# The last norm's residual added on GpSimd and VectorE, and the background work of a fused block re-laned

## The chip, the cores and the metric

The kernel runs on one core of a Trainium2 chip. The metric is the device time of one execution, in microseconds (us); the kernel before has a median of 2214.71 us over three runs (2211.72 to 2218.50). TensorE is called PE in the views of the profile, VectorE DVE, ScalarE ACT, GpSimd POOL, and SyncE, which issues most of the transfers, SP. An engine's name with a "q" behind it is its sequencer, and "L252" is line 252 of the kernel before.

## The reference

One layer over 2048 tokens of 1024 channels, in float32:

```
h = rmsnorm(x, norm_mix_pre)
u_pool, u_glu, g_a, g_b = split(h @ w_in)                 # 512, 2 x 512, 1024, 1024 columns
A = (pool_mixer(u_pool) * pool_scale) @ w_pool_out        # trailing means over 2/4/8/16 frames minus the frame,
                                                          # a 128x128 map per group
v = causal_depthwise_conv(a * sigmoid(gate), width 31) + conv_b
B = silu(layernorm(v, conv_ln_g, conv_ln_b)) @ w_conv_out
merged = sigmoid(g_a) * A + sigmoid(g_b) * B
x = x + rmsnorm(merged @ w_o, norm_mix_post)
h = rmsnorm(x, norm_mlp_pre)
f = square(relu(h @ w_up)) @ w_down                       # 4096 hidden channels
out = x + rmsnorm(f, norm_mlp_post)
```

## The kernel before

**Tiles.** Channels lie on the 128 partitions. The tokens are two halves (b = 0 and 1) of 1024, each of two blocks of 512 (t = 0 and 1). A *cell* is a tile of 128 partitions by 1024 columns: 512 tokens of two groups of 128 channels. A cell has 512 KB, and so has one operation's tile of weights.

**Matmuls.** Each float32 operand is split into a rounded part and a rest (`split`, `split_w`: a cast on ScalarE, a subtraction on VectorE), and three of the four products of parts are made. The large matrix products run as *octets*: eight block products are replaced by seven (forms i = 1 to 7), whose operands are sums and differences of weight tiles (`weight_parts`) and of cells (`token_parts`). One *product* is one form: 24 matmuls of 128 x 128 by 512, some 5.4 us of PE. Its `sink` takes the result out of one of three PSUM tiles, which `ps_mm` hands round.

**Order of the work.** The products are PE's main line. Everything else is background: generators (the convolution's 31 taps, LayerNorm, pooling, the norms' sums, the last weights) sit in `Lane`s. After each product `bg()` calls each lane once. A lane adds its rate to a credit and takes one generator step per unit; a bare `yield` ends a step, `yield n` ends the lane's turn and lets it pass over n - 1 further calls. So the rates and the numbers behind `yield` say how many products later a step is issued. The instructions' final order and the buffers are chosen by a scheduler of priorities: `tc.high_priority(offset)` lifts instructions ahead of others, and `behind()` ties a lane's instructions behind the main line. On each engine the instructions then run in that fixed order; SP's and POOL's transfers wait in it for what they depend on.

**Octets ahead.** `run_octets` goes through the jobs (octet, form), the first two octets interleaved as `START` says. Before each product it asks for the token parts of a later job with `parts.need`: the next one for the first four jobs, then two jobs ahead.

**Pools of tiles.** `big` has 28 tiles for cells, accumulators and token parts; `tr` has nine, which sinks, lanes and splits share; `fo` has five in the later stages; `wr` has four for raw weights, `wh` and `wl` three each for their parts. Where a weight's rest was kept from the first half (`kept`), or was made ahead for the last slab (`lows`), it is loaded into `wl` rather than computed.

**The stages, by the profile's clock:** inputs, the first octet and the projections of b = 0 (to about 306 us), branch A, the projections of b = 1 (350 to 632), the merge and output projection of b = 0, branch A of b = 1, `mlp_up` of b = 0 (814 to 1124), merge and output projection of b = 1, `mlp_up` of b = 1 (to 1577), and the down projection of both halves, with the last norm. Within them:

- `conv_steps` and `pool_steps` of b = 0 run in the lane `tail`, then in the second projections' first lane, followed by `norm_steps(0, 1)`. `conv_steps` of b = 1 waits until both are through.
- `norm_steps(b, lag)` is the LayerNorm. It loads the four cells `yd`, subtracts the mean, stores each cell again, and sums the squares; after the root it loads all four a second time, scales them, applies the sigmoid and stores `zd`.
- `pool_weights` multiplies the pooling's maps into `w_pool_out`; the maps' two parts are the constant tiles `pw`.
- `mlp_scale` makes the second norm's scale: it loads `x1d`, squares on ScalarE, adds on VectorE, and `root_acc` on PE sums over partitions (L458). Its lane runs beside `last_weights` in `mlp_up` of b = 1.
- The last norm has one `Finish` object per (b, t). `steps` squares the finished cells, `root_pe` and `root_dve` give the inverse root, `spread_pe` spreads it over partitions into `rb`; then each cell is multiplied by `rb` and x (`x1d`, in DRAM) is added. For b = 0 a POOL-issued transfer with `accum_op` adds `x1d` into the cell, and SP stores it. For (1, 1) two cells go that way and two have x loaded by `fetch` and added on VectorE. For (1, 0), in `at_end`, two outputs start as copies of `x1d` and get the cell added by a transfer into DRAM; the other two are added on VectorE, the last in halves.

The core of the way by transfer:

```
mul(two(y), two(y), per_token(self.rb))
...
nc.gpsimd.dma_start(y, x1d[self.b, c, self.t], accum_op=ALU.add)
load(out[self.b, c, self.t], y)
```

Of the kernel before, what the change touches and what calls it, by code (L numbers as in the profile page):

```python
# [15 lines left out]
P = 128  # L16
# [8 lines left out]
CW = 512  # L25
# [43 lines left out]
def block_kernel(  # L69
# [23 lines left out]
    p_wr = pool("pwr", 4)  # L93
# [838 lines left out]

    def norm_steps(b, lag):
# [21 lines left out]
        for c in range(CC):  # L955
# [3 lines left out]
            load(yd[b, c, 0], y[c])  # L959
# [14 lines left out]
        prefetch(0)  # L974
        yield 1
        sg = {}
        for c in range(CC + 1):
            if c < CC:
                if c + 1 < CC:
                    prefetch(c + 1)  # L980
# [8 lines left out]
            if c:  # L989
                mul(y[c - 1], y[c - 1], sg[c - 1])  # L990
                load(zd[b, c - 1, 0], y[c - 1])
            yield 1

    pw = [p_const.tile([P, CW], F32R, tag=f"pw{i}", name=f"pw{i}") for i in (0, 1)]
# [3 lines left out]
    def pool_weights():  # L998

        yield 2  # L1000
        raw = tr()
        load(raw[:, :CW], w_pool)
# [12 lines left out]
        for g, t in ahead_by_one(range(CC), get):  # L1015
            hi, lo = split(t, *TR)
            yield 3
# [354 lines left out]
    def mlp_scale(b, buf):  # L1372

        st = None
        for t in (0, 1):
# [10 lines left out]
            yield 1  # L1386
# [11 lines left out]
    def mlp_up(b, parts):  # L1398
        def one(u):
# [87 lines left out]
    def run(*octets):  # L1487
        run_octets([o for group in octets for o in group], bg)
# [5 lines left out]
    tail = Lane(1.3, conv_steps(0, (0,)))  # L1494
# [14 lines left out]

    def more():  # L1510
# [3 lines left out]
        tail.rate = 3  # L1514
# [3 lines left out]
    lanes.append(tail)  # L1518
    then(lambda: lanes.append(stats), o2, 5)
    run(  # L1520
        [o2],
        [then(more, pi, 3)],
        gate(0, parts, 3, sad, "ga", "lows"),
        gate(0, parts, 5, sbd, "gb", "sums"),
    )
# [21 lines left out]
    def pooling():  # L1547
        lanes[0].rate = 2.8
        lanes.append(Lane(1.4, marked(pool_steps(1, False), "pool")))
# [9 lines left out]
        gate(1, parts, 5, sbd, "gb", "sums"),  # L1559
    )  # L1560
# [33 lines left out]
    run(octs)  # L1594
# [191 lines left out]

    class Finish:
# [28 lines left out]
        def steps(self, lag):  # L1816
# [6 lines left out]
            if self.b and self.t:  # L1823
                self.fetch(self.order[2:])
# [12 lines left out]
            self.left = list(self.order)  # L1837
# [3 lines left out]
        def mul_left(self, n=4):  # L1841
            for c in self.muls[:n]:
                y = self.ready[c]
                mul(two(y), two(y), per_token(self.rb))
                if c not in self.x:
                    nc.gpsimd.dma_start(y, x1d[self.b, c, self.t], accum_op=ALU.add)
                    load(out[self.b, c, self.t], y)
                    self.left.remove(c)
            self.muls = self.muls[n:]
            self.add_left(0)  # L1850

        def add_left(self, n):
            for c in self.left[:n]:
                add(self.x[c], self.x[c], self.ready[c])
                load(out[self.b, c, self.t], self.x[c])
            self.left = self.left[n:]

        def first_squares(self):
# [207 lines left out]
```

## Time and profile before

| | |
|---|---|
| median of three runs | 2214.71 us (2211.72 to 2218.50) |
| the profiled execution | 2215.49 us |
| its span, first to last instruction | 2213.7 us |
| mean granted TensorE clock | 0.990 |
| PE busy | 2165.7 us, 9556 matmuls |
| VectorE, ScalarE, GpSimd busy | 1677.5, 1040.2, 20.6 us |
| transfers | 567.51 MB, mean 256 GB/s |

A row of the waits reads: engine, tile and line that waited, then what ended the wait, then total us, times and the longest. A row of the windows reads: stretch, its length, busy time and number of instructions of PE, weight load, VectorE, ScalarE and GpSimd, the mean granted clock, the transfers' busy share and GB/s. A row of the timeline reads: start, length, engine, line, operation, tiles out<-in, shape and how many were merged. Times are counted from the span's start.

### The profile page before, as it was taken

What the parts mean: (1) busy time and instruction counts of PE and PEld (TensorE: products, weight loads), DVE (VectorE), ACT (ScalarE), POOL (GpSimd) and SP (SyncE); (2) the same over time, 40 slices, a digit from 0 to 9 for tenths busy, and PEclk for the clock granted to TensorE, in tenths of its full rate; (3) what the DMA queues carried; (4) which work ended last, traced back from release to release, by engine and by line L of the source; (5) the groups of instructions that cost most, each with busy time, mean ns of one, the idle gap of its engine ahead of it and who ended that gap; (6) DMA issues with size and microseconds to landing.
All of it is one profiled execution on the core that took longest, in us unless ns stands there. A gap on an engine that the chain in (4) does not pass through costs nothing.

```text
span 2213.7 us, 25020 instructions
## 1 busy us (share of the span) xinstructions
PE 2165.7 (98%) x9556; PEld 1784.4 (81%) x9556; DVE 1677.5 (76%) x1633; ACT 1040.2 (47%) x1098; POOL 20.6 (1%) x39
## 2 busy tenths in 40 slices
PE   9999999999999999999999999999999999999996
PEld 7788787887888788888888877888888888888875
DVE  8998998987778888967657856876754656696667
ACT  5444353334533445456535766664554222223553
POOL 0000000000000000000000000000000000000001
PEclk9999999999999999999999999999999999999998
DMA  4779897678986688365686677985966545446798
GB/s 166 275 291 344 305 366 282 236 278 310 351 323 238 252 311 310 123 218 189 229 306 236 247 267 266 329 317 197 372 213 233 181 156 189 149 146 219 266 319 248
DMA packets 162791, 567.51 MB, mean 256 GB/s; under 512 B 18896, under 2 KB 23120, under 8 KB 162640
## 3 DMA queue, kind: packets, MB, share of 16 engines
q1 hardware_dynamic: 145968, 505.09, 64.1%
q10 hardware_dynamic: 12672, 46.14, 5.3%
q0 software_dynamic: 4032, 14.68, 2.5%
q8 instruction: 75, 1.23, 0.2%
q14 instruction: 44, 0.36, 0.0%
HBM read 376.49 MB, written 190.41 MB: 256 GB/s over the span
## 4 chain that ended last, share of the span: by engine, by line
PE 76%; DVE 9%; DMA 9%; issue 2%; ACT 2%; SPq 0%; DVEq 0%; ACTq 0%; POOL 0%; POOLq 0%
PE down L252 26%; PE up L252 22%; PE glu L252 6%; PE wo L252 6%; PE B L252 4%; PE A L252 4%; PE ga L252 3%; PE gb L252 3%; PE pool L252 2%; DVE y L918 2%; DVE wl L123 1%; DMA tr<-yd 1%; DVE tr L120 1%; DMA fo<-x1d 1%; DMA kept<-ws 1%
## 5 line engine op out<-in xcount | busy, mean ns | idle before, releaser
L252 PE MATMUL up<-big,wh 128*128 128x512 f32 x1792 | 482.4, 390 | 2.1 <-DVE big L123 1.8
L252 PEld LDWEIGHTS up<-big,wh 128*128 128x128 f32 x1792 | 337.0, 188 | 74.5 <-DVE big L123 3.9
L209 ACT CAST wh<-wr 128x1024 fp32r<-128x1024 f32 x169 | 177.5, 1051 | 324.1 <-PE up L252 77.8
L252 PE MATMUL down<-tr,wh 128*128 128x512 f32 x800 | 311.7, 390 | 0.0
L918 DVE SCALAR_TENSOR_TENSOR y<-v,cst,y 128x1024 f32<-128x1024 f32 x240 | 307.3, 1281 | 2.8
L252 PE MATMUL down<-fo,wh 128*128 128x512 f32 x784 | 301.8, 390 | 0.0
L252 PE MATMUL up<-big,wl 128*128 128x512 f32 x896 | 277.2, 390 | 0.0
L252 PE MATMUL down<-fo,wl 128*128 128x512 f32 x768 | 236.8, 390 | 2.9 <-DMA wl<-lows 2.9
L209 ACT CAST wh<-ws 128x1024 fp32r<-128x1024 f32 x118 | 124.2, 1052 | 221.8 <-PE up L252 84.1
L252 PEld LDWEIGHTS up<-big,wl 128*128 128x128 f32 x896 | 168.3, 188 | 34.7
L120 DVE TENSOR_TENSOR big<-big,down 128x1024 f32<-128x1024 f32 x88 | 106.8, 1218 | 111.9 <-PE down L252 104.0
L1727 ACT CAST fo<-tr 128x1024 fp32r<-128x1024 f32 x86 | 86.8, 1051 | 210.0 <-PE down L252 132.1
L252 PEld LDWEIGHTS down<-tr,wh 128*128 128x128 f32 x800 | 150.6, 188 | 31.2
L252 PEld LDWEIGHTS down<-fo,wh 128*128 128x128 f32 x784 | 147.5, 188 | 30.6
L252 PEld LDWEIGHTS down<-fo,wl 128*128 128x128 f32 x768 | 144.1, 188 | 33.2 <-DMA wl<-lows 3.3
L123 DVE TENSOR_TENSOR wl<-ws,wh 128x1024 fp32r<-128x1024 f32 x110 | 134.2, 1220 | 32.7 <-ACT wh L209 31.5
L123 DVE TENSOR_TENSOR wl<-wr,wh 128x1024 fp32r<-128x1024 f32 x99 | 120.5, 1218 | 27.9 <-ACT wh L209 26.8
L123 DVE TENSOR_TENSOR tr<-tr,fo 128x1024 fp32r<-128x1024 f32 x86 | 101.8, 1220 | 46.5 <-ACT fo L1727 46.5
L252 PE MATMUL wo<-big,wh 128*128 128x512 f32 x480 | 128.9, 390 | 0.0
L252 PE MATMUL gb<-big,wh 128*128 128x512 f32 x448 | 121.0, 392 | 3.0 <-DVE tr L120 2.4
L252 PE MATMUL glu<-big,wh 128*128 128x512 f32 x432 | 120.2, 400 | 3.5 <-DVE big L123 1.8
L252 PE MATMUL ga<-big,wh 128*128 128x512 f32 x448 | 120.9, 392 | 0.0
(197 smaller groups left out, 3349.1 us busy)
## 6 DMA issues: line engine op xcount, KB each, us to landing
tr<-fd SPq DMA_DIRECT2D x110, 512.0 KB, 4.6
wl<-kept SPq DMA_DIRECT2D x81, 512.0 KB, 4.8
kept<-wl SPq DMA_DIRECT2D x74, 512.0 KB, 5.7
wr<-w_down SPq DMA_DIRECT2D x68, 512.0 KB, 5.2
wr<-w_up SPq DMA_DIRECT2D x64, 512.0 KB, 4.6
wr<-w_in SPq DMA_DIRECT2D x56, 512.0 KB, 5.4
fd<-tr ACTq DMA_DIRECT2D x54, 512.0 KB, 3.6
fd<-tr SPq DMA_DIRECT2D x48, 512.0 KB, 3.5
```

What stands on the lines that cost most here:

```text
L120: return nc.vector.tensor_tensor(o, a, b, op=ALU.add)
L123: return nc.vector.tensor_tensor(o, a, b, op=ALU.subtract)
L209: nc.scalar.copy(hi[:, :n], src[:, :n])
L252: i = nc.tensor.matmul(ps, w[wp][:, (at + k) * P : (at + k + 1) * P], rhs[k][xp], start=start and n == 0, stop=stop and n == len(order) - ...
L918: nc.vector.scalar_tensor_tensor(acc, v[:, k : k + TB], wk, acc, op0=ALU.mult, op1=ALU.add)
L1727: nc.scalar.copy(hi, t)
```

## The change

1. *Last norm.* Every cell of the last norm now has x loaded by `fetch` on SP. Thirteen of the sixteen adds are `beside`, a GpSimd `tensor_tensor`; three are VectorE's (`order[1]`, `order[2]` and the halves of `order[3]` of (1, 0)). No transfer adds. For b = 0 the stores are issued by GpSimd, for b = 1 by SP.
2. *LayerNorm.* The last two cells, `HELD`, stay in their `tr` tiles between the two passes: they are neither stored nor loaded again, and the second pass begins with them. It asks for up to two cells ahead instead of one.
3. *Raw weights.* `wr` has five tiles. `pw` moves from the constants into a `tr` tile that `pool_weights` holds.
4. *Scale roots.* `mlp_scale` yields 2 instead of 1 between the sum and `root_acc`.
5. *Lanes.* `run_octets` asks three jobs ahead (from the fifth job, or from the fourth in the last `mlp_up`); the convolution's lane starts a product later at rate 1, `more` comes two forms later at rate 2.5; the second projections' lanes get rates 3.6 and 1.0; LayerNorm b = 1 has lag 3; `conv1` goes at 2.8; `pool_weights` waits 4; the last norm of b = 0 has rate and lag 3. The MLP sink's add is lifted by 60. `ahead[0]`, the lift of weight loads, is raised to 260 after `o2`'s first form.

```
-    p_wr = pool("pwr", 4)
+    p_wr = pool("pwr", 5)
...
-    def run_octets(octets, bg):
+    def run_octets(octets, bg, early):
...
-            o.run(i, jobs[min(n + (2 if n > 3 else 1), len(jobs) - 1)][1], bg)
+            o.run(i, jobs[min(n + (3 if n > early else 1), len(jobs) - 1)][1], bg)
...
+    HELD = (CC - 2, CC - 1)
     def norm_steps(b, lag):
...
-            load(yd[b, c, 0], y[c])
+            if c not in HELD:
+                load(yd[b, c, 0], y[c])
...
-        prefetch(0)
+        order = HELD + tuple(c for c in range(CC) if c not in HELD)
+        ready = list(HELD)
+
+        def ask(n):
+            if n < CC and order[n] not in ready:
+                prefetch(order[n])
+                ready.append(order[n])
+
+        ask(0)
         yield 1
         sg = {}
-        for c in range(CC + 1):
-            if c < CC:
-                if c + 1 < CC:
-                    prefetch(c + 1)
+        for n in range(CC + 1):
+            if n < CC:
+                c = order[n]
+                ask(n + 1)
+                ask(n + 2)
                 mul(y[c], y[c], r)
...
-    pw = [p_const.tile([P, CW], F32R, tag=f"pw{i}", name=f"pw{i}") for i in (0, 1)]
...
     def pool_weights():
...
         raw = tr()
+        both = mk(*TR, F32R)
+        pw = both[:, :CW], both[:, CW:]
...
             hi, lo = split(t, *TR)
-            yield 3
+            yield 4
...
     def mlp_scale(b, buf):
...
             ss = sq.total()
-            yield 1
+            yield 2
...
             def sink(m, t, ps, s):
...
-                    mark(add(o, ps, s))
+                    with tc.high_priority(offset=60):
+                        mark(add(o, ps, s))
...
-    tail = Lane(1.3, conv_steps(0, (0,)))
+    tail = Lane(1, conv_steps(0, (0,)))
...
+    def after_glu():
+        ahead[0] = AHEAD
+        lanes.append(tail)
...
     def more():
...
-        tail.rate = 3
+        tail.rate = 2.5
...
-    lanes.append(tail)
     then(lambda: lanes.append(stats), o2, 5)
     run(
-        [o2],
-        [then(more, pi, 3)],
+        [then(after_glu, o2, 1)],
+        [then(more, pi, 5)],
...
     def pooling():
...
-        lanes[0].rate = 2.8
-        lanes.append(Lane(1.4, marked(pool_steps(1, False), "pool")))
+        lanes[0].rate = 3.6
+        lanes.append(Lane(1.0, marked(pool_steps(1, False), "pool")))
...
-    conv1.gens.append(norm_steps(1, 2))
+    conv1.gens.append(norm_steps(1, 3))
...
     def faster():
...
-        conv1.rate = 3.4
+        conv1.rate = 2.8
...
+    def beside(o, a, b):
+        return nc.gpsimd.tensor_tensor(o, a, b, op=ALU.add)
...
-        def finish(self, c):
+        def finish(self, c, aside=False):
             y = self.ready[c]
             mul(two(y), two(y), per_token(self.rb))
-            if c in self.x:
-                x = self.x[c]
-                i = add(x, x, y)
-                load(out[self.b, c, self.t], x)
-                return i
-            else:
-                nc.gpsimd.dma_start(y, x1d[self.b, c, self.t], accum_op=ALU.add)
-                load(out[self.b, c, self.t], y)
+            x = self.x[c]
+            if aside:
+                beside(x, x, y)
+                (nc.gpsimd, nc.sync)[self.b].dma_start(out[self.b, c, self.t], x)
+                return
+            i = add(x, x, y)
+            load(out[self.b, c, self.t], x)
+            return i
...
         def steps(self, lag):
...
-            if self.b and self.t:
-                self.fetch(self.order[2:])
+            self.fetch(self.order[: 4 if self.b else 2])
...
-                for c in self.order:
-                    self.finish(c)
+                for n, c in enumerate(self.order):
+                    self.finish(c, True)
+                    self.fetch(self.order[n + 2 : n + 3])
                     yield
...
         def mul_left(self, n=4):
...
+                self.finish(c, True)
...
         def first_squares(self):
...
-            for c in self.order[:2]:
-                load(out[self.b, c, self.t], x1d[self.b, c, self.t])
-            for c in self.order[2:]:
-                self.x[c] = mk(*BIG)
-                load(self.x[c], x1d[self.b, c, self.t])
+            self.fetch(self.order)
...
         def at_end(self):
...
-                    fin[1, 1].add_left(1)
...
-                with behind():
-                    fin[1, 1].mul_left()
-                    fin[1, 1].add_left(4)
-                for c in self.order[:2]:
-                    y = self.ready[c]
-                    done = mul(two(y), two(y), per_token(self.rb)).ins
-                    nc.gpsimd.dma_start(out[self.b, c, self.t], y, accum_op=ALU.add)
+                self.finish(self.order[0], True)
+                self.finish(self.order[1])
                 done = self.finish(self.order[2]).ins
...
-    run(octs)
+    run(octs, early=2)
...
-                lanes += [Lane(2, fin[0, 1].steps(2), fin[0, 0].steps(2))]
+                lanes += [Lane(3, fin[0, 1].steps(3), fin[0, 0].steps(3))]
```

More of the change, by code (lines that the diff above doesn't have):

```diff
@@ L988, in norm_steps @@
                 )
-            if c:
-                mul(y[c - 1], y[c - 1], sg[c - 1])
-                load(zd[b, c - 1, 0], y[c - 1])
+            if n:
+                c = order[n - 1]
+                mul(y[c], y[c], sg[c])
+                load(zd[b, c, 0], y[c])
             yield 1
-    pw = [p_const.tile([P, CW], F32R, tag=f"pw{i}", name=f"pw{i}") for i in (0, 1)]
     w_pp = [dram("wpp", (P, D)) for _ in range(CPS)]
@@ L1485, in empty, with run @@
         lanes.clear()
-    def run(*octets):
-        run_octets([o for group in octets for o in group], bg)
+    def run(*octets, early=3):
+        run_octets([o for group in octets for o in group], bg, early)
     parts = Parts(first_parts)
@@ L1513, in more @@
         tail.gens.append(chain_of(pool_steps(0, True), conv_steps(0, (1, 2, 3), False)))
-        tail.rate = 3
+        tail.rate = 2.5
     pi = pool_in(0, parts, ahead_raw[1])[0]
     ahead[0] = 45
-    lanes.append(tail)
     then(lambda: lanes.append(stats), o2, 5)
     run(
-        [o2],
-        [then(more, pi, 3)],
+        [then(after_glu, o2, 1)],
+        [then(more, pi, 5)],
         gate(0, parts, 3, sad, "ga", "lows"),
         gate(0, parts, 5, sbd, "gb", "sums"),
+        early=3,
     )
@@ L1559, in block_kernel @@
         gate(1, parts, 5, sbd, "gb", "sums"),
+        early=3,
     )
@@ L1586, in block_kernel @@
     conv1.rate = 0.9
-    conv1.gens.append(norm_steps(1, 2))
+    conv1.gens.append(norm_steps(1, 3))
     lanes.append(conv1)
     def faster():
-        conv1.rate = 3.4
+        conv1.rate = 2.8
     octs = mlp_up(0, parts)
     then(faster, octs[1])
-    run(octs)
+    run(octs, early=3)
     empty()
@@ L1842, in mul_left @@
             for c in self.muls[:n]:
-                y = self.ready[c]
[L1844 to L1848, printed above, removed]
-            self.muls = self.muls[n:]
[L1850 to L1856, printed above, removed]
+                self.finish(c, True)
+            self.muls = self.muls[n:]
         def first_squares(self):
@@ L1933, in fill_cells, with filler @@
             fill[i] = token_cells(0, i, 0, (p_fo, "fo"))
-    def filler(part):
+    def filler(part, halves):
         for i in FIRST:
-            for o in (0, 1):
+            for o in halves:
                 w = part(i, o)
@@ L1958, in block_kernel @@
     lanes += [Lane(1, chain)]
-    filler(weights_down(0))
+    fw = weights_down(0)
+    filler(fw, (0, 1))
     octs = mlp_up(1, parts)
```

3 lines of the change are left out of this document (removed).

## The prediction

> **What bounds the kernel now.** I read the page first (busy shares and the chain that ended last), then what TensorE (PE) waited for, then the stretches around those waits, then the last 30 us.
>
> ```profile
> span 2213.7 us, 25020 instructions
> PE 2165.7 (98%) x9556; PEld 1784.4 (81%) x9556; DVE 1677.5 (76%) x1633; ACT 1040.2 (47%) x1098; POOL 20.6 (1%) x39
> PE 76%; DVE 9%; DMA 9%; issue 2%; ACT 2%; SPq 0%; DVEq 0%; ACTq 0%; POOL 0%; POOLq 0%
> ```
>
> PE is busy for 98% of the span, so 48 us are idle. The matmuls are not touched: the change can only move those 48 us, and what idle time does to the clock. The second view lists PE's waits, cause, total, times, longest:
>
> ```profile
> PE rb L458 <- DVE fo L120: 4.7, 3, 1.6
> PE glu L252 <- DMA wl<-kept: 4.0, 1, 4.0
> PE down L252 <- DMA wl<-lows: 2.9, 1, 2.9
> PE gb L252 <- DVE tr L120: 2.4, 2, 2.0
> PE up L252 <- DVE big L123: 1.8, 3, 0.8
> PE glu L252 <- DVE big L123: 1.8, 1, 1.8
> PE rb L458 <- DVE sm L120: 1.7, 1, 1.7
> PE glu L252 <- ACT big L202: 1.2, 1, 1.2
> ```
>
> They are a dozen separate causes; no engine but PE is a bound over the whole run. The third view gives stretches (us; PE busy; ... granted clock):
>
> ```profile
> 95.00:111.00 16.00, 12.75 (x42) 9.30 (x41) 14.66 (x14) 10.26 (x12) 0.00 (x0) 0.79 0.87 340
> 256.00:268.00 12.00, 9.97 (x37) 7.72 (x36) 11.96 (x11) 3.17 (x3) 0.00 (x0) 0.86 0.67 244
> 360.00:374.00 14.00, 9.98 (x37) 7.78 (x36) 8.96 (x8) 2.82 (x4) 0.00 (x0) 0.88 0.82 298
> ...
> 1365.00:1377.00 12.00, 10.39 (x43) 8.17 (x43) 8.81 (x8) 6.96 (x7) 0.00 (x0) 0.86 0.81 299
> ...
> 2126.00:2138.00 12.00, 9.08 (x34) 6.98 (x33) 2.33 (x3) 2.85 (x3) 0.00 (x0) 0.86 1.03 384
> ...
> 600.00:650.00 50.00, 50.00 (x222) 41.42 (x221) 35.94 (x31) 20.60 (x21) 0.00 (x0) 1.00 0.89 329
> ```
>
> The undisturbed row has 222 matmuls in 50 us, 4.44 per us. A stretch's loss is its idle time plus (1 - clock) times its length. 256 to 268: 2.0 idle + 0.14 x 12 = 1.7, so 3.7 us; by the count, 12 - 37/4.44 = 3.7 as well. In the same way 95 to 111 lost 3.25 + 3.4 = 6.6, 360 to 374 lost 4.0 + 1.7 = 5.7, 2126 to 2138 lost 2.9 + 1.7 = 4.6. So a wait of 2 us can cost 4: some waits take the clock down behind them.
>
> The Trainium skill's "TensorE: Matmul & The Clock Gate", in its table of why this matters, sets the limit at idle gaps of about 3 us; the trace disagrees, since the 2.0 us gap at 256 to 268 was followed by a clock of 0.86. By that rule only the 4.0 us wait would carry a clock term, and the sum below would come to some 2203 us.
>
> **The change part by part.**
>
> *Scale roots a call later* (`mlp_scale`, second `yield 2`). PE reaches `root_acc` before VectorE has finished the sum: 4.7 us in three waits, of at most 1.6 each; one took the clock down (1365 to 1377: 0.14 x 12 = 1.7). Together 6.4 us. One call is one product of 24 matmuls, 24/4.44 = 5.4 us, more than the longest wait. What is late next: the sum's `fo` buffer (one of five) comes free 5.4 us later, and the other lane's loads on SyncE (SP) queue behind that. Between 0 and -6.4 us; I take -5.5, near the full gain, because 5.4 covers 1.6 three times over.
>
> *Fifth raw weight buffer.* SP issues in order; its waits, and its issues ahead of the 4.0 us wait:
>
> ```profile
> SPq L129 <- ACT wh L209: 61.4, 56, 4.4
> SPq L129 <- DMA big<-x1d: 34.5, 8, 7.3
> ```
>
> ```profile
> 356.56 0.32 SPq L129 DMA_DIRECT2D wr<-kept  x1
> ...
> 359.40 0.32 SPq L129 DMA_DIRECT2D wr<-kept  x1
> 359.76 3.79 SPq L129 DMA_DIRECT2D wl<-kept  x3
> ```
>
> The `wl<-kept` that PE waits for stands on SP behind a `wr<-kept`, which waits until ScalarE's cast frees a raw buffer. With five buffers that load takes the one freed before 356.56, so the `wl` load goes out some 2.8 us earlier (359.40 - 356.56). That leaves about 1.2 of the 4.0 us, too little by the rows above to take the clock down. Gain 2.8 + 1.7 = 4.5; ends 0 (another wait on SP takes its place) and -5.7; I take -4. The buffer's memory is that of `pw`, which becomes a `tr` tile held during `pool_weights`; of that, the rivals.
>
> *Last norm of the first half* (`finish`, b = 0). The chain there:
>
> ```profile
> 2109.42 2.27 DVE big L126 x2
> ...
> 2112.43 10.64 DMA big<-x1d
> ...
> 2123.56 8.78 DMA wl<-lows
> ```
>
> An adding transfer takes 10.64 us, SP's store of its result waits for it, and `wl<-lows` behind that store comes 2.9 us late: 4.6 us lost. After the change the add is GpSimd's (POOL), and its store stands on POOL's queue, so SP is rid of the 34.5 us of waits above. What SP gets instead are the plain loads of x (`fetch`, two early, then one per step), which wait only for a `big` tile. Of 28, 16 are accumulators by then, 2 are `u`, 3 hold cells: free ones remain, so I cost these loads at nothing; if the cover goes, they block SP as the stores did. Ends 0 and -4.6; I take -4. `Lane(3)` and `steps(3)` move the same steps by a call or two, cost nothing while PE has products, and give the sums more time.
>
> POOL's price: no POOL arithmetic of this size is in the trace. Its nearest rows:
>
> ```profile
> L616 POOL CAST ident<-tr 128x128 fp32r<-128x128 f32 x1 | 0.3, 291 | 0.1
> ...
> L170 POOL MEMSET inv_d<- 128x1 f32 x1 | 0.1, 98 | 0.0
> ```
>
> (291 - 98)/128 = 1.5 ns a column; 1024 columns with one input 0.1 + 1.54 = 1.6 us, with two inputs up to twice that, 3.2. I estimate 2.4, the middle. There are 13 such adds (all four cells of three of the four `Finish`, one of the last), 31 us of an engine that is busy for 20.6 of 2213.7 us: hidden, except in the tail. The Trainium skill's "GPSIMD Engine Reference", section 3.1, has 4497 ns for twice the columns, so by estimate 2.3 us; the sum would be the same.
>
> *The tail.* After the last product VectorE works alone:
>
> ```profile
> 2188.46 2.35 DVE L126 TENSOR_TENSOR big<-big,rb 128x1024 f32<-128x1024 f32 x2
> 2190.72 1.22 DVE L120 TENSOR_TENSOR big<-big,big 128x1024 f32<-128x1024 f32 x1
> ...
> 2194.50 1.22 DVE L120 TENSOR_TENSOR big<-big,big 128x1024 f32<-128x1024 f32 x1
> 2195.67 3.48 DVE L126 TENSOR_TENSOR big<-big,rb 128x1024 f32<-128x1024 f32 x3
> 2199.19 1.22 DVE L120 TENSOR_TENSOR big<-big,big 128x1024 f32<-128x1024 f32 x1
> ...
> 2201.53 1.28 DVE L120 TENSOR_TENSOR big<-big,big 128x512 f32<-128x512 f32 x2
> ```
>
> ```profile
> 2189.26 1.95 PE L458 MATMUL rb<-inv_d,tr 128*128 128x1 f32 x16 [0.38 <-ACT tr L1889]
> ```
>
> ```profile
> 2208.00:2210.00 2.00, 0.00 (x0) 0.00 (x0) 0.00 (x0) 0.00 (x0) 0.00 (x0) 0.50 1.02 328
> 2210.00:2212.00 2.00, 0.00 (x0) 0.00 (x0) 0.00 (x0) 0.00 (x0) 0.00 (x0) 0.50 0.42 162
> ```
>
> ```profile
> DMA to landing us min/median/max: 4.0/9.2/11.6
> ```
>
> ```profile
> q1 hardware_dynamic: 1787, 6.65, 49.9%
> q0 software_dynamic: 818, 2.96, 43.9%
> ```
>
> The adds at 2190.72 and 2194.50 go to POOL; the first stood ahead of the root, which can begin when PE's sum is there (2189.26 + 1.95 = 2191.2) instead of at 2191.9: -0.7. The second ran while VectorE waited for PE's spread: nothing. Behind the root one add is new (order[1]): +1.1. VectorE ends some 0.4 us later, at 2203.2. The transfers, though, work at full share until about 2211, 8 us after VectorE's end at 2202.8: that backlog sets the end. From 2180 on the adding queue (q0) took 43.9% of 33.7 us for 2.96 MB, 5.0 us a MB, and the plain one (q1) 49.9% for 6.65 MB, 2.5 us a MB. Four adding transfers (0.52 MB each) and two copies of x1d leave; four plain loads and two plain stores come, and the other loads and stores stay. By these prices 10.5 + 2.6 us of transfer time go from the last 40 us and 7.9 come. So the last stores should land in 5 us (row: 4.0 at least, 9.2 at the median): at 2208.2 instead of 2202.8 + 9.3 = 2212.1. Ends +0.4 and -5; I take -4, near the fast end, as the backlog is what the change removes. POOL's five last adds fit: two by 2189, two by 2194.5, the last from 2196.8 to 2199.2; at 3.2 us each to 2200.3, still ahead of VectorE.
>
> *Parts and lanes in the first 300 us.* `run_octets` asks for token parts three jobs ahead from the fifth job on, not two: form 7, whose cells came late at 95 to 111, is asked for one job (5.4 us) earlier. By the lanes' rates, counted call by call, the convolution's first cell ends two calls later and its second not before the next input stage: some 17 taps fewer on a VectorE that is busy for 14.66 of 16 and 11.96 of 12 us there. They land where it is busy for some 36 of 50. At stake: 6.6 + 3.7, and the later `up<-big` waits of 1.8: 12. I take half, -6; ends 0 and -12.
>
> *LayerNorm keeps two cells.* Four 512 KB stores and four loads go away over both halves. PE waits for the LayerNorm only at its root (`sm`, 1.7 us), which follows the first pass, whose loads all stay: 0. `steps`, `in_stats` and the pool weights otherwise keep their instructions; `high_priority(60)` in the sink and the longer lags (LayerNorm 3, pool weights 4) order them differently: 0.
>
> *New waits.* The order from 55 to 1060 us is dealt out anew. I take +6, half of the largest of the groups above, with 0 and +13 as ends.
>
> Sum: -5.5 - 4 - 4 - 4 - 6 + 6 = -17.5 us. The profiled execution took 2215.5 us, its span and 1.8 around it, 0.8 above the median of 2214.7. 2215.5 - 17.5 = 2198.0, less 0.8: **2197 us**, 0.8% faster.
>
> **The rivals.** *The port.* VectorE's instructions with two inputs in SBUF might stand still while POOL adds. For it: in the tail two POOL adds fall on the root's small steps and one on the add of order[1]. The steps would wait from 2191.2 to 2192.0 and, where POOL's next add goes first, to 2194.4: 0.8 to 3.2 us, say 2. The add of order[1], due at 2198, would wait for POOL's to end at 2199.2: 1.2. The backlog's gain is then eaten: tail 0 instead of -4, elsewhere hidden under PE. 2201 us. No row of before shows POOL arithmetic beside VectorE. The Trainium skill's "SBUF — State Buffer", section "Who interferes with whom", states this rule (an exclusive lock against a GpSimd instruction that reads SBUF); no run here shows it yet.
>
> *A reshuffle.* The waits close where named, and as many open elsewhere: +18 instead of +6. For it: the waits of before have a dozen causes, none shared. Against: four are closed by construction. 2209 us, or no change.
>
> *Slower: `tr` runs out.* Nine `tr` tiles serve the sinks and the lanes. `pw` now holds one during `pool_weights` (about 20 calls), and the LayerNorm two over its lags (4 calls for b = 0, 10 for b = 1). If a sink finds none, its PSUM tile stays full, and PE stops: an idle time of 2 us costs 3.7 (256 to 268). From about seven such stops on (6.6 + 17.5 = 24 us) it decides; a stop in every third of those 34 calls, eleven, gives 2197 + 41 = 2238 us. Against it: the gap at 256, with `pool_weights` running, ended on VectorE's backlog rather than on a tile.
>
> **How the numbers follow.** About 0.3% (6.6 us) is what a measurement here tells from no change. Forecast 0.40, port 0.24, reshuffle 0.21, `tr` 0.15. Of the forecast and the port 0.63 is faster; the reshuffle splits toward no change: faster 0.65, same 0.20, slower 0.15. All gains at their ends with no new waits: 2214.7 - 6.4 - 5.7 - 4.6 - 5 - 12 = 2181. The range 2180 to 2217 leaves out most of the `tr` case and little below.
>
> **What would show it.** Right: no PE wait on `fo` at L458, none on `wl<-lows` in the first half's last norm, the `wl<-kept` wait under 1.5 us, fewer clock dips before 300 us; no adding transfer; last store landing within 6 us of VectorE's end. Wrong: PE waits on sinks' `tr` tiles around 150 to 250 or 900 to 1000 us; SP waiting for `big` tiles ahead of `wl`; VectorE's root chain, 2.6 us long before (2191.9 to 2194.5), stretched by POOL.

## The result, and the profile after

The changed kernel takes 2191.75 us in the median of four runs (2190.13 to 2191.93), the kernel before 2213.22 (four runs): a ratio of 0.9902, 95% interval 0.9884 to 0.9920, or 21.5 us less. Forecast were 2197 us, 17.5 less. A second measurement of the same kernel (`ctl_after`) gave 0.9914 (0.9897 to 0.9931), with six runs from 2189.4 to 2198.0. Below, 0.9908 stands for the change, the mean of the two.

The page of the profiled execution, which took 2191.9 us (span, busy shares, the chain that ended last):

```profile
span 2190.1 us, 25018 instructions
PE 2157.9 (99%) x9556; PEld 1782.2 (81%) x9556; DVE 1690.8 (77%) x1632; ACT 1039.3 (47%) x1098; POOL 46.0 (2%) x48
PE 87%; DVE 6%; DMA 4%; issue 2%; ACT 1%; SPq 1%; DVEq 0%; ACTq 0%
```

PE idles for 32 us instead of 48. Another 8 us are in its busy time, 2157.9 for 2165.7 with the same 9556 matmuls: the clock dips less. On the chain, transfers fall from 9% to 4%. PE's waits now (cause, total, times, longest):

```profile
PE rb L550 <- DVE sp L530: 5.1, 2, 3.3
PE rb L458 <- DVE tr L120: 3.6, 4, 1.2
PE glu L252 <- ACT tr L408: 2.9, 1, 2.9
...
PE down L252 <- ACT fo L1746: 1.1, 1, 1.1
...
PE down L252 <- DVE big L123: 0.8, 1, 0.8
PE rb L458 <- DVE sm L120: 0.7, 1, 0.7
```

The three largest that the prediction priced (`fo` at L458, `wl<-kept` and `wl<-lows`) are gone, but for 0.3 us of `wl<-kept` at another place. PE now waits longest for the spread of a root, for a sum of squares, and for ScalarE's copy of a PSUM tile (L408, in `held`). These are the rows of the same causes before; the first of them, 3.7 us on `tr`, is missing from the list in the prediction:

```profile
PE rb L458 <- DVE tr L120: 3.7, 3, 2.2
...
PE rb L550 <- DVE sp L530: 1.4, 2, 1.2
...
PE glu L252 <- ACT tr L408: 0.2, 1, 0.2
```

So the copy's wait is new, the spread's has grown, and the sum's is as long as it was. Next come the stretches that the prediction priced, a new one, and two where the sinks might have lacked `tr` tiles (columns as before; the eighth number, ahead of the two on transfers, is the clock). The changed kernel reaches the same matmuls earlier, by 2 us at 256 and by 20 at 2126, so the second to fifth stretches are moved by that much:

```profile
95.00:111.00 16.00, 15.20 (x59) 11.76 (x60) 15.07 (x15) 8.96 (x11) 0.00 (x0) 0.91 0.85 329
254.00:266.00 12.00, 12.00 (x54) 9.95 (x53) 11.82 (x11) 6.06 (x6) 0.00 (x0) 1.00 0.84 276
355.00:369.00 14.00, 14.00 (x63) 11.60 (x62) 7.38 (x6) 4.80 (x5) 0.00 (x0) 1.00 0.96 351
1350.00:1362.00 12.00, 12.00 (x59) 10.03 (x58) 10.58 (x10) 6.53 (x7) 0.00 (x0) 1.00 0.89 333
2105.00:2117.00 12.00, 12.00 (x58) 10.06 (x57) 11.86 (x10) 4.24 (x5) 4.00 (x4) 1.00 1.02 416
2156.00:2168.00 12.00, 9.60 (x42) 7.47 (x41) 8.31 (x16) 2.40 (x3) 5.29 (x3) 0.86 0.44 180
150.00:250.00 100.00, 100.00 (x443) 82.78 (x442) 84.39 (x88) 47.05 (x53) 0.00 (x0) 1.00 0.93 337
900.00:1000.00 100.00, 100.00 (x442) 82.80 (x441) 85.09 (x73) 55.10 (x56) 0.00 (x0) 1.00 0.43 160
```

Of the five that had lost time, four are undisturbed: full clock, and no idle time of PE. The first still loses 0.8 us of idle time and 0.09 x 16 = 1.4 of clock, and 2.9 us of idle time now lie just ahead of it. In the last two rows PE does not stop.

By the start of each stage's first matmul, the profiled time went thus. "Last matmul" is the last one of the last product of the down projection.

| from, to | before | after | difference |
|---|---|---|---|
| start, branch A of b = 0 | 306.7 | 300.6 | -6.1 |
| branch A, and two `pool` products of b = 1 | 54.4 | 55.7 | +1.3 |
| the other projections of b = 1 | 270.8 | 264.1 | -6.6 |
| B of b = 0 to the start of `mlp_up` of b = 1 | 624.3 | 622.1 | -2.1 |
| `mlp_up` of b = 1 | 320.4 | 312.0 | -8.4 |
| down projection, to the start of the last matmul | 610.3 | 612.3 | +2.0 |
| last matmul to the end | 26.8 | 23.3 | -3.6 |

The spans differ by 23.6 us: the profiled execution of before, 2215.5 us, stands 2.3 above the median of its four runs.

**The tail, and the port.** VectorE's instructions in the last 40 us (start, length, line, operation, tiles):

```profile
2152.64 2.99 DVE L502 TENSOR_SCALAR sy<-sa 128x4 int32<-128x4 int32 x1
...
2171.41 0.76 DVE L126 TENSOR_TENSOR s<-s,q 128x4 f32<-128x4 f32 x1
2172.20 2.29 DVE L500 TENSOR_SCALAR sa<-s 128x4 f32<-128x4 f32 x1
2174.53 0.17 DVE L502 TENSOR_SCALAR sy<-sa 128x4 int32<-128x4 int32 x1
...
2176.51 0.16 DVE L123 TENSOR_TENSOR sq<-sy,sp 128x4 fp32r<-128x4 f32 x1
2178.54 3.48 DVE L126 TENSOR_TENSOR big<-big,rb 128x1024 f32<-128x1024 f32 x3 [1.88 <-PE rb L550]
...
2185.59 1.28 DVE L120 TENSOR_TENSOR big<-big,big 128x512 f32<-128x512 f32 x2
```

and POOL's adds in the same time, then all of them in one group (total, mean ns):

```profile
2153.18 2.42 POOL L1807 TENSOR_TENSOR big<-big,big 128x1024 f32<-128x1024 f32 x1
...
2169.77 4.69 POOL L1807 TENSOR_TENSOR big<-big,big 128x1024 f32<-128x1024 f32 x2 [2.15 <-ACT tr L1894]
2179.90 2.36 POOL L1807 TENSOR_TENSOR big<-big,big 128x1024 f32<-128x1024 f32 x1 [5.43 <-issue]
```

```profile
L1807 POOL TENSOR_TENSOR big<-big,big 128x1024 f32<-128x1024 f32 x13 | 31.4, 2430 | 1337.2 <-DVE big L126 1323.2 <-issue 11.8 <-ACT tr L1894 2.1
```

In the kernel before, the first of the long steps was as short as its neighbours:

```profile
2192.24 0.17 DVE L500 TENSOR_SCALAR sa<-s 128x4 f32<-128x4 f32 x1
```

Lay the two timelines side by side. A step on four columns, 0.17 us before, took 2.29 us at 2172.20 and ended at 2174.49, when POOL's pair of adds ended (2169.77 + 4.69 = 2174.46). The one at 2152.64 ended at 2155.63, POOL's add there at 2155.60. So the root's chain in the tail lasts 5.5 us (2171.2 to 2176.7) where it took 2.7 before (2191.9 to 2194.6). The multiplications by `rb`, which have one input in PSUM, run at 3.48/3 = 1.2 us throughout. This is the rule of the Trainium skill's "SBUF — State Buffer", section "Who interferes with whom", and the trace agrees, for the one-input TENSOR_SCALAR as well as for the TENSOR_TENSOR of two SBUF inputs.

PE pays once more. It waits 3.3 us for the root, and the eight matmuls that spread it then take 1.9 us (2176.62 to 2178.5) where they took 1.1 before, and take 1.1 in `x_four` (below), where the wait is 0.6. The first of the eight in the changed kernel, then in `x_four`:

```profile
2176.62 0.39 PE L550 MATMUL rb<-ident,sp 128*128 128x128 f32 x1 [3.27 <-DVE sp L530]
```

```profile
2178.72 0.30 PE L550 MATMUL rb<-ident,sp 128*128 128x128 f32 x1 [0.56 <-DVE sp L530]
```

The stores make up for it. Transfers issued after 2182 (count, size, median us to landing):

```profile
out<-big SPq DMA_DIRECT2D x3, 512.0 KB, 2.8
out<-big SPq DMA_DIRECT2D x2, 256.0 KB, 2.1
```

VectorE ends 20.0 us after the start of the last matmul (2186.87 - 2166.86) instead of 15.9, which is +4.1: the root starts 0.6 earlier, its chain takes 2.7 more, the spread 0.8, and the one add more 1.2. From there to the end of the span it is 3.25 us (2190.12 - 2186.87) instead of 10.9, which is -7.6. Together -3.5.

### The profile page after: what moved, and what is told of

Read it like the earlier page. It is cut to its first block, busy times and chain, and to the rows that moved or that the text cites. A ratio compares the mean times of both kernels' runs of the same rounds, so it can differ in the third digit from the quotient of the medians.

```text
span 2190.1 us, 25018 instructions
## 1 busy us (share of the span) xinstructions
PE 2157.9 (99%) x9556; PEld 1782.2 (81%) x9556; DVE 1690.8 (77%) x1632; ACT 1039.3 (47%) x1098; POOL 46.0 (2%) x48
## 4 chain that ended last, share of the span: by engine, by line
PE 87%; DVE 6%; DMA 4%; issue 2%; ACT 1%; SPq 1%; DVEq 0%; ACTq 0%
PE up L252 27%; PE down L252 26%; PE wo L252 7%; PE ga L252 6%; PE glu L252 5%; PE B L252 4%; PE A L252 4%; PE gb L252 3%; PE pool L252 3%; DMA kept<-ws 1%; DVE tr L120 1%; DVE y L918 1%; DMA tr<-yd 1%; PE rb L458 1%; DVE wl L123 1%
## 5 line engine op out<-in xcount | busy, mean ns | idle before, releaser
L209 ACT CAST wh<-wr 128x1024 fp32r<-128x1024 f32 x169 | 177.7, 1052 | 324.9 <-PE up L252 85.2
L209 ACT CAST wh<-ws 128x1024 fp32r<-128x1024 f32 x118 | 124.2, 1053 | 216.2 <-PE up L252 92.0
L123 DVE TENSOR_TENSOR wl<-ws,wh 128x1024 fp32r<-128x1024 f32 x110 | 134.1, 1219 | 52.0 <-ACT wh L209 50.8
L123 DVE TENSOR_TENSOR tr<-tr,fo 128x1024 fp32r<-128x1024 f32 x86 | 101.8, 1219 | 42.4 <-ACT fo L1746 42.4
L123 DVE TENSOR_TENSOR wl<-wr,wh 128x1024 fp32r<-128x1024 f32 x99 | 120.4, 1217 | 10.9 <-ACT wh L209 8.8
```

The lines of the kernel that those rows point to most:

```text
L123: return nc.vector.tensor_tensor(o, a, b, op=ALU.subtract)
L209: nc.scalar.copy(hi[:, :n], src[:, :n])
```

## The experiments

Each ratio is against the kernel before on the same chip, so the changed kernel is the base at 0.9908 in all but `b_wr5`. An interval is some ±0.002, 4 us. The changed kernel itself ran on the same chip only with `x_copy`, `x_lag` and `x_all` (as `ctl_after`); for the other runs the ratio carries the base over from chip to chip.

| run | edit | median us | ratio (95%) | ratio less 0.9908, in us |
|---|---|---|---|---|
| `u_roots` | scale roots as before | 2198.64 | 0.9949 (0.9929 to 0.9969) | +9 |
| `u_wr4` | four raw buffers | 2213.26 | 1.0012 (1.0002 to 1.0022) | +23 |
| `u_norm` | last norm as before | 2196.31 | 0.9942 (0.9921 to 0.9962) | +8 |
| `u_lanes` | first lanes as before | 2206.28 | 0.9981 (0.9968 to 0.9994) | +16 |
| `u_ahead2` | parts two jobs ahead | 2193.34 | 0.9929 (0.9910 to 0.9948) | +5 |
| `u_held` | LayerNorm keeps none | 2198.69 | 0.9956 (0.9943 to 0.9969) | +11 |
| `x_four` | POOL's adds before the root | 2192.16 | 0.9918 (0.9898 to 0.9938) | +2 |
| `x_lag` | and b = 0's last norm earlier | 2199.56 | 0.9937 (0.9922 to 0.9952) | +6 |
| `x_copy` | `x_four`, copies lifted | 2186.34 | 0.9882 (0.9866 to 0.9898) | -6 |
| `x_all` | all three | 2196.79 | 0.9928 (0.9914 to 0.9943) | +4 |
| `b_wr5` | before, with five raw buffers | 2204.85 | 0.9981 (0.9969 to 0.9994) | (4 us faster than before) |

Taken out singly, six parts lose 72 us between them, of a gain of 20. They are not terms of a sum: what a part is worth depends on which others are there.

**Five raw buffers.** In the changed kernel:

```
-    p_wr = pool("pwr", 5)
+    p_wr = pool("pwr", 4)
```

> The changed kernel with four raw weight buffers instead of five. If the fifth buffer is what lets SP issue the kept weights' loads in time, the wait of PE on wl<-kept comes back in the second input projections (near 350 to 370 us), 4 us with a dip of the clock: 2191.8 + 5 = 2197 us. Rival: the new lanes alone took that wait away; then 2192 us, no wait on wl<-kept over 1 us, while SP's waits for ScalarE's casts grow by several us that nobody feels.

The whole gain is gone, but not where I had put it: from the pooling to the second `ga` this kernel takes 114.2 us, as the changed kernel does, and PE has no wait on `wl<-kept` over 0.3 us: the other edits close that wait without the buffer. It loses in the first run (+6), in `mlp_up` of b = 0 (+7) and of b = 1 (+7). Its waits on the copies of L408 are 16.9 us in all, 3.3 in the changed kernel; the largest row:

```profile
PE up L252 <- ACT tr L408: 7.7, 3, 3.9
```

and the chain that ended last around one of them (start, length, what):

```profile
862.37 10.88 DMA kept<-ws
...
873.26 1.24 DVE ws L123
...
875.48 1.04 ACT wh L209
876.52 0.92 ACT tr L408
...
877.48 4.60 PE up L252 x19
```

A store to DRAM (`kept<-ws`) takes 10.9 us. A sum on VectorE waits for it, a weight's cast on ScalarE for that sum, and behind the cast, in ScalarE's fixed order, stands the copy of a PSUM tile (L408) that PE needs back. No compute engine waits for a raw buffer at that moment; SP does, 9.5 us for the same sum, which reads one. The fifth buffer changes the order of the issues; that the casts' inputs thereby come earlier was not shown, and `ctl_after`, which has five buffers, has the same chain once (below). In the kernel before, the same edit alone:

```
-    p_wr = pool("pwr", 4)
+    p_wr = pool("pwr", 5)
...
-    pw = [p_const.tile([P, CW], F32R, tag=f"pw{i}", name=f"pw{i}") for i in (0, 1)]
...
+        both = mk(*TR, F32R)
+        pw = both[:, :CW], both[:, CW:]
```

> The kernel before with the fifth raw weight buffer alone (and the pooling maps in a tr tile, which pays for it). In the changed kernel, going back to four buffers cost some 20 us rather than the 4 predicted, and not at the wait that was named. If the buffer is worth that by itself, because ScalarE's PSUM copies stand behind casts whose raw weights come late, this run gains much of it: about 2197 us. Rival: the other edits ask for weights earlier and need the fifth buffer, which by itself is worth the 4 us of the prediction or nothing: 2207 to 2212 us.

Two of the stretches in this kernel:

```profile
1365.00:1377.00 12.00, 12.00 (x55) 9.94 (x53) 10.79 (x10) 8.74 (x10) 0.00 (x0) 1.00 0.58 206
360.00:374.00 14.00, 14.00 (x63) 11.43 (x62) 10.96 (x9) 4.06 (x5) 0.00 (x0) 1.00 0.99 385
```

The wait at 360 to 374 is gone, as forecast, and so are the waits on `fo` at 1365, which I had put down to the scale roots: `mlp_up` of b = 1 takes 313.9 us here instead of 320.4. So each of the two, the buffer alone and the other edits without it, closes the wait at 360. A new wait of 3.4 us on L408, at 167, gives part of it back.

**Scale roots as before.**

```
-            yield 2
+            yield 1
```

> The changed kernel with one edit undone: the scale roots are issued at once again (second yield of mlp_scale back to 1). If the later call is what hides the sums, PE waits on fo at L458 come back, some 4.7 us of idle time and one dip of the clock: 2191.8 + 6 = 2198 us, and the stretch from the first up product of b = 1 to the first down product is 6 us longer than with the change. Rival: the new order of the lanes hides the sums by itself; then 2192 us and no such waits.

`mlp_up` of b = 1 takes 312.8 us in its profile, 0.8 more than in the changed kernel, with a single wait on `fo` of 0.4 us: the waits did not come back. The time came out as expected all the same, but not by the path expected: the medians are 6 us above `x_four` on the same chip. The stages of the profiled execution, 4.8 us longer in all, differ both ways: 4.0 more in `mlp_up` of b = 0, where PE, VectorE and ScalarE have the order of the changed kernel, 1.8 more in the down projection, 4.6 less in the projections of b = 1. What the edit is worth, and by what path, stays open.

**Last norm as before.** `Finish`, its lane's rate and its lag are those of the kernel before:

```
-                lanes += [Lane(3, fin[0, 1].steps(3), fin[0, 0].steps(3))]
+                lanes += [Lane(2, fin[0, 1].steps(2), fin[0, 0].steps(2))]
```

> The changed kernel with the last norm as before (adding transfers, SP stores, rate and lag 2), all other edits kept. If the adds on GpSimd and the plain loads are worth what the tail and the wl<-lows wait cost, this run is 4 us longer between the last product and the end and waits again for wl<-lows: 2199 us. Rival, the port: VectorE lost about as much to GpSimd's adds (some 12 us of VectorE time, of which some 6 stood on the path) as the transfers cost; then 2192 to 2195 us, a shorter root chain (2.7 us instead of 5.5 us), and no wait of PE on that root's spread beyond 1.2 us.

The wait that the change removes is back:

```profile
PE down L252 <- DMA wl<-lows: 2.9, 1, 2.9
```

The tail takes 27.6 us instead of 23.3, the down projection 613.9 instead of 612.3. So this part is worth 4.3 + 1.6, some 6 us by the profile. With the adding transfers back, the last stores land late again (issued after 2180; median us to landing):

```profile
out<-big SPq DMA_DIRECT2D x5, 512.0 KB, 10.5
...
out<-big SPq DMA_DIRECT2D x2, 256.0 KB, 10.2
```

And without POOL's adds PE does not wait for the spread of (1, 1).

**POOL's adds before the root.** All four adds of (1, 1) go to POOL ahead of the root's steps:

```
             self.muls = list(self.order)
-            self.mul_left(2)
+            self.mul_left(4)
```

> The changed kernel, with all four products with the inverse root of (1, 1) made at once when the root is there, in the 3.4 us in which VectorE sits idle before the last product ends, instead of two then and two after it. GpSimd's third and fourth adds thereby end some 2 us earlier. If GpSimd's adds hold up VectorE's small root steps through a shared port, the last root takes some 3.3 us instead of 5.5, and the kernel ends 2 us earlier: 2190 us. Rival: the long TENSOR_SCALAR of 2.3 us there is a wait for something else (a semaphore, its first use); then it stays, and the time is 2192 us.

VectorE's steps at the root, and POOL's adds:

```profile
2176.42 0.17 DVE L500 TENSOR_SCALAR sa<-s 128x4 f32<-128x4 f32 x1
...
2178.61 0.16 DVE L123 TENSOR_TENSOR sq<-sy,sp 128x4 fp32r<-128x4 f32 x1
```

```profile
2166.88 9.38 POOL L1807 TENSOR_TENSOR big<-big,big 128x1024 f32<-128x1024 f32 x4 [6.34 <-issue]
```

POOL is through at 2176.26, the chain takes 2.7 us again, and from the last matmul to the end it is 19.8 us instead of 23.3. The root starts 4.35 us after the last matmul in both kernels, so the two multiplications that the edit moves as well were off the path. That isolates the port's price in the tail: 3.5 us, 2.7 of the chain and 0.8 of the spread. The time does not show it, as the profiled execution lost 3.4 us in the down projection: about 2.2 at its start (642 matmuls from 1550 to 1700 instead of 652; the same two waits of 1.2 and 0.8 us are followed by a clock of 0.88 over 14 us here, of 1.00 in the changed kernel), and 1.2 in a deeper dip of the clock (0.71 instead of 0.83 from 2160 to 2170) behind the wait of 1.8 us on the spread of (1, 1) that both kernels have.

**The last norm of b = 0 earlier**, to take POOL's adds away from that of (1, 1) as well (on top of `x_four`):

```
-                lanes += [Lane(3, fin[0, 1].steps(3), fin[0, 0].steps(3))]
+                lanes += [Lane(3, fin[0, 1].steps(2), fin[0, 0].steps(2))]
```

> The changed kernel with the four products of (1, 1) at once, and the last norm's steps of the first half issued with a lag of 2 products, not 3, so that GpSimd's adds of the first half should be over before the root of (1, 1) near 2152 us. If the port holds up that root (its TENSOR_SCALAR of 3.0 us) and PE waits 3 us for its spread, the wait goes and the root of the end is short too: 4 to 5 us less than the control. Rival: the adds fall on other VectorE work that PE waits for; then no better than 2 us less than the control, from the last root alone.

The rival was right. PE's largest row of waits, then VectorE and POOL around the longest one:

```profile
PE rb L458 <- DVE tr L120: 8.7, 5, 5.8
```

```profile
2140.84 2.50 DVE L123 TENSOR_TENSOR tr<-tr,fo 128x1024 fp32r<-128x1024 f32 x1 [0.88 <-ACT fo L1746]
2143.27 3.49 DVE L123 TENSOR_TENSOR tr<-tr,big 128x1024 fp32r<-128x1024 f32 x1
...
2153.48 4.54 DVE L120 TENSOR_TENSOR big<-big,big 128x1024 f32<-128x1024 f32 x2
```

```profile
2152.57 3.24 POOL L1807 TENSOR_TENSOR big<-big,big 128x1024 f32<-128x1024 f32 x1 [5.92 <-issue]
```

Two adds that take 1.2 us each take 4.54 together, and POOL's 3.24 instead of 2.4. Two subtractions, 1.2 us each otherwise, took 2.50 and 3.49 beside POOL's adds at 2139.84 and 2143.26. Together VectorE, which does not stop from there on, loses 5.7 us; PE waits 5.8 us for the sum of squares behind. Moved off one chain, the adds fell on another.

**The first lanes as before** (the rates, `tail`, `more`, the LayerNorm's lag, and weight loads lifted by 45 only until `more`):

```
-    tail = Lane(1, conv_steps(0, (0,)))
+    tail = Lane(1.3, conv_steps(0, (0,)))
...
-        lanes[0].rate = 3.6
-        lanes.append(Lane(1.0, marked(pool_steps(1, False), "pool")))
+        lanes[0].rate = 2.8
+        lanes.append(Lane(1.4, marked(pool_steps(1, False), "pool")))
```

> The changed kernel with the lanes' rates, starts and LayerNorm's lag of before, and with weight loads lifted by 45 only until the pooling octet's third form, all else kept (five raw buffers, three jobs ahead, the last norm, two cells held). If the thinner lanes are what relieves VectorE in the first projections, the matmuls up to branch A start 5 to 6 us later than with the change, and the wait on wl<-kept near 360 us may come back, since four raw buffers instead of five did not bring it back: 2191.8 + 6 to 10 = 2198 to 2202 us. Rival: asking three jobs ahead did it; then 2192 us and a first run as with the change.

The first run takes 315.7 us to branch A instead of 300.6, more than before the change (306.7). Two of its stretches, 165 to 177 and 296 to 308, each hold a wait for ScalarE, 3.4 us (L408) and 3.6 (L209), and have a mean clock of 0.72. `b_wr5`, with the old rates and five raw buffers, has the first of these waits but not the second, and reaches branch A at 308.7; so it is the old rates together with other parts of the change that cost 15 us. Which part was not tried.

**Parts two jobs ahead.**

```
-            o.run(i, jobs[min(n + (3 if n > early else 1), len(jobs) - 1)][1], bg)
+            o.run(i, jobs[min(n + (2 if n > 3 else 1), len(jobs) - 1)][1], bg)
```

> The changed kernel, asking for token parts two jobs ahead as before, all else kept. If the earlier request is what shortened the wait for form 7 near 95 to 111 us and the up waits near 1265 to 1290 us, these come back: 3 us in the first run, 2 us in mlp_up of b = 1, so 2197 us. Rival: the lanes did it; then 2192 us.

PE's order is unchanged. At 102.9 a wait of 2.2 us for `big` (L123) is back, the late cells that the prediction named, and two of 0.8 in `mlp_up` of b = 1; the first run is 1.8 us longer, that `mlp_up` 3.4. The intervals overlap, so the size, some 2 to 5 us, is not settled.

**LayerNorm keeps no cells.**

```
-    HELD = (CC - 2, CC - 1)
+    HELD = ()
```

> The changed kernel with no cell held in LayerNorm: all four are stored and loaded again, 4 MB more of transfers, and asking two cells ahead stays. Predicted worth of the held cells: 0, as PE waits only for the root that comes before: 2192 us. Rival one: the 4 MB delay what stands behind them on the full queues near 500 to 580 and 950 to 1050 us, by way of casts and copies behind late loads: 2195 us or more. Rival two: holding two of nine tr tiles costs; then it is faster, below 2189 us.

```profile
PE rb L458 <- DVE sm L120: 5.3, 1, 5.3
```

In the changed kernel this wait is 0.7. The load of the third cell is issued at 527.4, behind the first cell's store on SP, instead of 522.4. So the stores stand between the first pass's loads, and taking two away moves the root. That stretch, the projections of b = 1, is 5.2 us longer; the rest of the 11 us lies in later stages and was not traced.

**The copies lifted** (with `x_four`), after `u_wr4` had shown them waiting behind casts:

```
-            mark(nc.scalar.copy(s, ps))
+            with tc.high_priority(offset=300):
+                mark(nc.scalar.copy(s, ps))
```

> The changed kernel with the four products of (1, 1) at once, and ScalarE's PSUM copies (L408) lifted by 300 ahead of casts. If PE's waits on these copies come from casts that stand ahead of them on ScalarE and wait for late weights, the waits on L408 go (2.9 us near 95 us, and those near 290, 511 and 868 us): 3 to 6 us less than the control, 2187 us. Rival: the casts that fall behind are then late for PE in their turn; the time is that of the control or 2 to 5 us more, with new waits on wh or wl.

**The changed kernel again**, beside it: no edit.

> The changed kernel as it is, on the same chip as the next three, to see how far chip and execution move it: 2190 to 2195 us, with a profile whose waits agree with the first one to within 3 us at each place, apart from waits that end on ScalarE's PSUM copies (L408), which came and went near 868 us between runs of the same order of instructions.

Waits of the control, then of the kernel with both edits:

```profile
PE up L252 <- ACT tr L408: 3.2, 2, 3.0
...
PE glu L252 <- ACT tr L408: 2.5, 1, 2.5
```

```profile
PE pool L252 <- DVE wl L123: 1.8, 1, 1.8
...
PE ga L252 <- ACT tr L409: 1.1, 1, 1.1
```

It takes 2186.3 us (2184.3 to 2188.7), 6.6 less than the control and faster than either kernel. PE waits for its copies 1.1 us at most. At 95 us the waits that take their place, for the weights of `pool`, eat the gain; what stays is the tail of `x_four` and `mlp_up` of b = 0 (308.5 us, 313.4 in the control). The control's wait of 3.0 us there has the chain of `u_wr4`: a store of 10.1 us from 849.85 on, then a sum, a cast, and the copy at 863.23. It is not there in every execution: with the same order of instructions the changed kernel's first profile has 0.2 us in its place, and takes 308.3 us. So the order decides that PE can wait for a store's landing, and the landing decides whether it does. What the lift is worth alone is not shown: of the 5.3 us between the two profiles 3.5 are the tail's, which `x_four` has too, and the rest is this wait that comes and goes.

**All three:**

```
+            with tc.high_priority(offset=300):
+                mark(nc.scalar.copy(s, ps))
...
+            self.mul_left(4)
...
+                lanes += [Lane(3, fin[0, 1].steps(2), fin[0, 0].steps(2))]
```

> All three together (four products at once, copies lifted by 300, lag 2 for the first half's last norm). If both theories hold, 7 to 10 us less than the control, 2183 us. Rival: the copies' lift costs what it gives; then as the kernel with the lag alone.

Up to the down projection it is 2.7 us ahead of the changed kernel; its down projection then takes 621 us instead of 612, with the waits of `x_lag`. The time is the rival's; what brings it is the lag, not the lift.

## Why the prediction was right, and where its terms were not

The direction and, to 4 us, the size were right; several terms were not. That their sum came so near is partly luck: what was missed in one place (the down projection, 2.0 us longer instead of 4 shorter) was made up in others (8.4 instead of 5.5 in `mlp_up` of b = 1, 6.6 instead of 4 in the projections of b = 1).

- *Parts and lanes, -6 to 300 us.* Measured -6.1, and 256 to 268 is clear. But undoing the lanes costs 16 us: with the old rates, other parts of the change bring new waits.
- *Scale roots, -5.5.* The waits are gone, and `mlp_up` of b = 1 gained 8.4 us. The cause was wrong: `b_wr5`, which has the old roots, lost the same waits and gained 6.5 of it; `u_roots` did not get them back. Failed is the step that let one call's delay alone remove them.
- *Fifth raw buffer, -4 at 360 to 374.* The wait went, all 4.0 us and its dip, and alone the buffer is worth 4 us; but `u_wr4`, without the buffer, does not have the wait either. And the buffer counts for the whole gain when it is taken out. The step treated a buffer as one wait on SP; taking it out moves some 90 of SP's 997 issues and 46 of ScalarE's 1098 instructions to other places in their order.
- *Last norm of the first half, -4.* The wait on `wl<-lows` went (-4.6), but the down projection is 2.0 us longer. New there: 1.9 us at its start (`down<-fo` and `down<-big`, of which `b_wr5` has both too), 3.6 in three waits around the root of (1, 1), and 1.7 of clock at 2156 to 2168. The middle one, 1.8 us for the spread, is the port's: the stretched step at 2152.64, 2.8 us too long, stands in that chain, and `u_norm`, without POOL's adds, has no such wait. "Hidden, except in the tail" was the failing step.
- *The tail, -4.* Measured -3.6 as a sum of two sizes that I had otherwise: VectorE +4.1 for +0.4, the landings -7.6 for -4.4. The port rival's mechanism was real; its price for the chain, 2 us of 0.8 to 3.2, was 2.7, and the slower spread, which it did not name, cost 0.8. Its second charge, 1.2 us for the add of `order[1]`, did not come: POOL's add was over at 2182.26, and the two adds at 2181.94 took 2.52. The rival did not decide, because the last stores land in 2.1 to 2.8 us, faster than the 4.0 that I took as the least.
- *POOL's price, 2.4 us of 1.6 to 3.2.* Measured 2.43, 31.4 us in all as forecast.
- *LayerNorm's cells, 0.* `u_held` lost 11 us. I had counted the loads of the first pass and overlooked the stores between them on SP; that accounts for 5.2 us of it.
- *New waits, +6.* In the place of the waits named came 2.9 us ahead of 95, 1.3 in branch A and the 7.2 of the down projection above: 11.4, for a term of +6.
- *The clock.* Shallow waits carried dips and went with them: a third of the 23.6 us is PE's busy time (-7.8), that is clock, and not idle time.
- *`tr` runs out.* PE is busy for all of 150 to 250 and 900 to 1000, so this rival was empty.

## What to carry to other kernels

Where a fixed order on each engine couples everything, price an edit by what its engine's queue does in it, and do not add single undo runs up: the buffer, the lanes and the kept cells each cost more to remove than their share. Before adds are moved to GpSimd, list VectorE's serial chains of small steps; put the adds before or after them, and check what they fall on next. Where PE waits for a PSUM copy, look at what stands ahead of the copy on its engine: the run with the copies lifted and the adds before the root was the fastest here, 6.6 us under the control.

## What was not expected of the hardware

- A step on 128 x 4 elements took 2.3 or 3.0 us instead of 0.17, until POOL's add ended; adds and subtractions of 128 x 1024 lost 1.3 to 2.3 us in the same way.
- At the end, stores of 512 KB landed in 2.8 us and of 256 KB in 2.1 where no adding transfer ran beside them; with the adding transfers back (`u_norm`) it was 10.5 and 10.2.
- The same order of instructions gave 0.2 or 3.0 us of wait at one place in two executions, and stages 5 us apart.
- The clock did not follow the wait's length alone: waits of 1.2 and 0.8 us were followed by a clock of 0.88 over 14 us in one kernel and by no dip in another with the same two waits, and one of 1.8 us by 0.84 over 11 us and by 0.69 over 11 us.
